# Six of eight head chunks for four output tiles inside the attention

## The chip, the cores and the metric

One core of a Trainium2 chip runs one launch of the kernel. The metric is device time in microseconds of that launch. TensorE (PE in the profile) multiplies, VectorE (DVE), ScalarE (ACT) and GpSimd (POOL) do the elementwise work, and SyncE (SP) issues nearly all transfers.

## The reference, cut to what matters

A transformer block over 512 tokens of width 1024, in float32. Sixteen heads of 64 are computed in two halves: eight "NSA" heads (a compressed, a selected and a window branch with gates) and eight heads with a window of 128 and a sink. Their outputs are joined, multiplied by an output matrix and normed into the residual; a gated MLP with a short convolution and a gated side input follow.

```python
h = rmsnorm(x, attn_pre_g)
proj = h @ w_in                                   # queries, keys, values, gates
o_nsa = nsa_attention(...)                        # heads 0..7,  (512, 512)
o_swa = swa_attention(...)                        # heads 8..15, (512, 512)
mix = concatenate([o_nsa, o_swa]) @ w_o           # (512, 1024) @ (1024, 1024)
x = x + rmsnorm(mix, attn_post_g)
h = rmsnorm(x, mlp_pre_g)
a, u = split(h @ w_gate_up)                       # 2 * 2816 columns
y = (gelu(causal_dwconv(a)) * u) @ w_down
x = x + rmsnorm(y, mlp_post_g)
x = x + (p @ w_ple) * sigmoid(x @ w_ple_gate)
```

The product with `w_o` is the one that the change touches: 8 tiles of 128 output features, each a sum over 8 chunks of 128 head dimensions (two heads).

## The kernel before, in words

Activations stand transposed, features on the partitions and the 512 tokens along the row. A float32 operand is split into a high and a low part, and every product of a 128x128 weight block with 128x512 activations takes three matmuls: high by high, high by low, low by high. A weight comes from memory through one of two raw buffers (`raw`, the transfer at line 133), ScalarE copies its high part (line 121), and VectorE or POOL subtracts for the low part (line 125). Converted weights live in six slots named `wh`, so three weights fit.

The attention runs in 16 units: eight NSA units (two groups of heads, four blocks of 128 queries each, in the order 3, 0, 2, 1) and then eight window units in the same order. Each step of the loop in `attention` computes the scores of unit `i` together with the product with the values of an earlier unit: of the unit before where that one is NSA, two back where it is a window unit. Its output is put into a pair of head chunks by `put_out`. So chunks 0 to 3 are complete at the end of step 8, chunks 4 and 5 at the end of step 13, and 6 and 7 after the last unit.

Into this go fillers: generators, each step of which is one chunk (three matmuls) of a product that can be done ahead. The attention's generators yield a nominal time in ns for each step; `fill` adds that time multiplied by a rate to a credit, and every 650 ns of credit (`FILL_STEP`) buys one filler step. The rate is taken from `RATES` by the kind of the unit: 0.36 for both NSA groups, 0.9 and 0.6 for the window groups. A filler's first matmul is pinned not to come earlier than an attention matmul six back (`LAG`). The fillers are the remaining projections (six of them, eight steps each) and then `out_proj_first`, which starts when step 8 is done: for all eight output tiles it multiplies chunks 0 to 3 (`mixmm`, lines 775 to 777) and ScalarE saves the sum (line 791). What is left when the units are over is run then. The order on each engine is worked out once by the framework's scheduler, from the program's order and its own timeline, and is fixed when the kernel runs.

`out_proj` adds the rest. For tiles 0 to 2, chunks 4 and 5 are multiplied first, since they cover the wait for the last unit's output, then chunks 6 and 7. Tiles 3 to 7 follow with one weight each, 512 columns (chunks 4 to 7), in PSUM tiles of the tag `mm`, which has two. VectorE adds each finished sum to the saved one (line 820), ScalarE squares it, POOL sums the squares; for the last tile VectorE does (line 230). At tile 2 the weights of the side input are loaded, at tile 4 the four input transfers of 512 KB (line 234), which SP issues in program order, and at tile 7 the first four gate-up weights. Then `norm_add` sets four tiles of the side product, column sums over the squares (line 201), two tiles, the transposition of the norm's factor, two more tiles; the MLP's first matmuls come behind them.

## Time and profile before

| What | us |
|---|---|
| median of 3 runs (lowest, highest) | 677.31 (676.53, 678.64) |
| the profiled execution | 677.48 |
| its span, first to last instruction | 675.7 |
| PE busy | 662.6 (98%) |
| PEld, weight loads, busy | 550.8 (82%) |
| DVE, ACT, POOL busy | 404.1, 324.8, 171.7 |

The granted TensorE clock is 0.998 of full speed over the span. Times in the rows are us from the span's start. In a row of the timeline the bracket holds the time that the engine sat idle before the instruction, and what released it. A matmul's own length overlaps the next one's, so distances between starts tell more than lengths. In names, `fill_` stands for fillers, `nsa_` and `swa_` for the two kinds of units, `outproj_` for the product behind the attention; the tiles of head chunks carry the names of the stage in which they were allocated.

### The profile page before, as it was taken

How to read it: one execution, taken by the hardware profiler on the slowest of the kernel's cores; microseconds unless marked ns; L12 is line 12 of the kernel's file. 1: busy time of each engine (PE TensorE's matmuls, PEld its weight loads, DVE VectorE, ACT ScalarE, POOL GpSimd, SP SyncE). 2: the span in 40 equal slices, each digit the busy share in tenths (PEclk: the TensorE clock that was granted, in tenths of full speed). 3: DMA queues.
4: the chain of work that ended last, by engine and by line, in shares of the span. 5: the costliest groups of instructions: out<-in, count | busy, mean ns of one | idle time of the engine just before them, and what ended most of it. 6: DMA issues, size and time to landing. Idle time of an engine off the chain costs nothing.

```text
span 675.7 us, 9173 instructions
## 1 busy us (share of the span) xinstructions
PE 662.6 (98%) x3273; PEld 550.8 (82%) x3273; DVE 404.1 (60%) x809; ACT 324.8 (48%) x602; POOL 171.7 (25%) x244
## 2 busy tenths in 40 slices
PE   8999999999999999999999999999999999999996
PEld 7988868877788777788888888888888888889985
DVE  6785877877657668668645455555542333324872
ACT  7554787877778555454333343433332322222341
POOL 1112577756656234312011110101010000001000
PEclk9999999999999999999999999999999999999999
DMA  8437523101122641122223222222233344232031
GB/s 296 169 105 226 158 63 78 33 16 49 48 83 99 233 146 63 64 93 95 99 107 105 95 94 93 94 94 95 96 97 103 116 121 136 86 99 82 1 124 63
DMA packets 24972, 69.55 MB, mean 103 GB/s; under 512 B 3168, under 2 KB 4448, under 8 KB 24928
## 3 DMA queue, kind: packets, MB, share of 16 engines
q1 hardware_dynamic: 24784, 68.89, 31.4%
q8 instruction: 26, 0.43, 0.3%
q14 instruction: 18, 0.15, 0.1%
q10 hardware_dynamic: 144, 0.08, 0.0%
HBM read 59.52 MB, written 2.10 MB: 91 GB/s over the span
## 4 chain that ended last, share of the span: by engine, by line
PE 89%; DVE 4%; ACT 3%; DMA 2%; issue 1%; ACTq 0%; DVEq 0%
PE mlpup_pss L144 5%; PE mlpup_pss L143 4%; PE mlpup_pss L140 4%; PE mlpup_psmm L143 3%; PE mlpup_psmm L140 3%; PE mlpup_psmm L144 3%; PE nsa_pso L541 3%; PE mlpup_pst L143 3%; PE mlpup_pst L140 3%; PE mlpup_pst L144 3%; PE mlpdown_pss L144 3%; PE mlpdown_pss L140 3%; PE mlpdown_pss L143 3%; PE nsa_pst L508 2%; PE mlpdown_psmm L140 2%; PE mlpdown_psmm L144 2%
## 5 line engine op out<-in xcount | busy, mean ns | idle before, releaser
L121 ACT ACTIVATE mlpup_wh<-mlpup_wr 128x1024 fp32r<-128x1024 f32 x40 | 42.5, 1063 | 82.2 <-PE mlpup_pss L143 30.3
L924 POOL TENSOR_TENSOR mlpup_s<-mlpup_s,r3b 128x512 f32<-128x512 f32 x22 | 29.4, 1339 | 186.6 <-ACT mlpup_s L923 186.6
L125 DVE TENSOR_TENSOR mlpdown_wh<-mlpdown_wr,mlpdown_wh 128x1024 fp32r<-128x1024 f32 (+1 forms) x28 | 33.1, 1181 | 59.8 <-ACT mlpdown_wh L121 59.8
L121 ACT ACTIVATE mlpdown_wh<-mlpdown_wr 128x1024 fp32r<-128x1024 f32 (+1 forms) x28 | 28.0, 1000 | 84.8 <-PE mlpdown_pss L143 33.1
L125 DVE TENSOR_TENSOR mlpup_wh<-mlpup_wr,mlpup_wh 128x1024 fp32r<-128x1024 f32 x40 | 50.6, 1265 | 9.2 <-ACT mlpup_wh L121 9.1
L140 PE MATMUL mlpup_pss<-r_u,mlpup_wh 128*128 128x512 f32 x120 | 46.8, 390 | 0.0
L144 PE MATMUL mlpup_pss<-r_u,mlpup_wh 128*128 128x512 f32 x120 | 46.7, 389 | 0.0
L143 PE MATMUL mlpup_pss<-r_u,mlpup_wh 128*128 128x512 f32 x120 | 46.7, 389 | 0.0
L530 POOL TENSOR_SCALAR nsa_u<-nsa_u,nsa_nrc,gate 128x512 f32<-128x512 f32 (+3 forms) x64 | 38.2, 607 | 22.5 <-DVE nsa_nrc L655 16.7
L624 ACT ACTIVATE nsa_u<-nsa_u,nsa_nnm 128x512 f32<-128x512 f32 (+3 forms) x64 | 35.5, 557 | 5.2 <-DVE nsa_nnm L620 4.9
L512 DVE TENSOR_TENSOR nsa_u<-nsa_pst,nsa_u 128x512 fp32r<-128x512 f32 (+1 forms) x43 | 29.0, 683 | 9.1 <-ACT nsa_u L510 8.8
L230 POOL TENSOR_TENSOR mlpdown_s<-mlpdown_s,mlpdown_s 128x512 f32<-128x512 f32 x6 | 7.8, 1298 | 100.4 <-ACT mlpdown_s L229 100.4
L620 DVE CUSTOM_DVE_ANT_0 nsa_u<-nsa_pss,biastables_u 128x512 f32<-128x512 f32 (+3 forms) x64 | 29.9, 486 | 5.3 <-PE nsa_pss L562 4.9
L125 POOL TENSOR_TENSOR fill_wh<-fill_wr,fill_wh 128x512 fp32r<-128x512 f32 (+1 forms) x14 | 24.7, 1762 | 32.9 <-ACT fill_wh L121 32.8
L144 PE MATMUL mlpdown_pss<-mlpup_u,mlpdown_wh 128*128 128x512 f32 (+1 forms) x88 | 32.0, 364 | 0.0
L140 PE MATMUL mlpdown_pss<-mlpup_u,mlpdown_wh 128*128 128x512 f32 (+1 forms) x88 | 32.0, 364 | 0.0
L143 PE MATMUL mlpdown_pss<-mlpup_u,mlpdown_wh 128*128 128x512 f32 (+1 forms) x88 | 32.0, 363 | 0.0
L510 ACT ACTIVATE nsa_u<-nsa_pst 128x512 fp32r<-128x512 f32 (+1 forms) x43 | 25.1, 592 | 13.0 <-PE nsa_pst L508 12.7
L923 ACT ACTIVATE mlpup_s<-mlpup_s 128x512 f32<-128x512 f32 x22 | 13.8, 633 | 36.2 <-DVE mlpup_s L922 36.2
L140 PE MATMUL mlpup_pst<-r_u,mlpup_wh 128*128 128x512 f32 x80 | 31.2, 390 | 0.0
L144 PE MATMUL mlpup_pst<-r_u,mlpup_wh 128*128 128x512 f32 x80 | 31.1, 389 | 0.0
L143 PE MATMUL mlpup_pst<-r_u,mlpup_wh 128*128 128x512 f32 x80 | 31.1, 389 | 0.0
(411 smaller groups left out, 1979.1 us busy)
## 6 DMA issues: line engine op xcount, KB each, us to landing
mlpup_wr<-in_gu_dram SPq DMA_DIRECT2D x40, 512.0 KB, 3.2
mlpdown_wr<-in_down_dram SPq DMA_DIRECT2D x16, 512.0 KB, 3.5
fill_wr<-in_win_dram SPq DMA_DIRECT2D x6, 512.0 KB, 3.6
mlpdown_wr<-in_down_dram SPq DMA_DIRECT2D x8, 384.0 KB, 3.1
fill_u<-fill_u SPq DMA_DIRECT2D x20, 128.0 KB, 2.4
loadx_u<-in_xT_dram SPq DMA_DIRECT2D x8, 256.0 KB, 4.8
compress_u<-projk_u SPq DMA_DIRECT2D x16, 128.0 KB, 2.3
fill_wr<-in_wo_dram SPq DMA_DIRECT2D x8, 256.0 KB, 2.9
```

Of the source, the lines that this page charges most:

```text
L121: h = nc.scalar.activation(hi, raw, AF.Copy)
L125: l = eng.tensor_sub(lw, raw, hi.bitcast(F32))
L140: r = self.pin(mm(ps, hi, x[:, 0, :], start=start, stop=False))
L143: mm(ps, lo, x[:, 0, :], start=False, stop=False)
L144: mm(ps, hi, x[:, 1, :], start=False, stop=stop)
L510: nc.scalar.activation(t[:rows, 0, :], pt[:rows], AF.Copy)
L512: nc.vector.tensor_sub(lo, pt[:rows], t[:rows, 0, :].bitcast(F32))
L530: self.nc.gpsimd.tensor_scalar(ap, ap, col, gate, op0=ALU.mult, op1=ALU.mult)
L541: self.att(nc.tensor.matmul(po, v, rhs, start=start, stop=stop))
L620: nc.vector.tensor_tensor_reduce(dst, src, dist, op0=ALU.add, op1=ALU.min, scale=SLOPES[8 + 4 * g + r], scalar=3e38, accum_out=nm[:, r, b ...
L624: nc.scalar.activation(dst, dst, AF.Exp, bias=nm[:, r, b : b + 1], scale=-1.0, accum_out=sm[:, r, b : b + 1])
L924: nc.gpsimd.tensor_mul(c0, c0, self.r3)
```

## The change

- A table `BORDER` gives the rates of steps 6, 7 and 8: 0.36, 0.7 and 0.9. Step 7 is the last NSA unit.
- `out_proj_first` takes a range of tiles and a number of chunks. Tiles 0 to 3 (`SIX` = 4) still take four chunks, from the end of step 8; tiles 4 to 7 take six, as a second filler that is appended at the end of step 13 (`NQT * 3 + 1`), when chunks 4 and 5 are complete. Weights of the second are 768 columns wide.
- In `out_proj`, tiles 4 to 7 multiply only chunks 6 and 7. Their weights, four times 256 columns, come in one transfer into one raw buffer when tile 4 is reached, are converted as one weight of 1024 columns, and each tile takes its part. `raw` lays the destination out in as many pieces as the source has.

```diff
--- before.py
+++ after.py
@@ -55,6 +55,8 @@
 FILL_STEP = 650.0
 WARM = 9
 RATES = [0.36, 0.36, 0.9, 0.6]
+BORDER = {6: .36, 7: .7, 8: .9}
+SIX = 4
 LAG = 6
 
 
@@ -130,7 +132,7 @@
 
     def raw(self, src, n=1024, tag="wr"):
         t = (self.wrp.tile([P, n], F32, tag="wr", name=self.nm("wr")) if tag == "wr" else self.u([P, n], F32, tag))
-        self.nc.sync.dma_start(t, src)
+        self.nc.sync.dma_start(t if len(src.shape) == 2 else t.rearrange("p (c n) -> p c n", c=src.shape[1]), src)
         return t
 
     def mm3(self, ps, wt, off, x, start, stop, keep=False):
@@ -743,7 +745,7 @@
                         self.drain(qf[f])
                 if mix[k] is None:
                     mix[k] = self.mix_tiles()
-                self.rate = RATES[k]
+                self.rate = BORDER.get(i, RATES[k])
                 u["mix"] = mix[k]
                 if u["kind"] == "n":
                     gens.append((self.nsa_scores(u), [(j + 1) / 8 for j in range(8)]))
@@ -758,13 +760,16 @@
                 self.mix = []
                 for k in range(2):
                     self.mix += [(mix[k][0][:, i, :], mix[k][1][:, i, :]) for i in range(2)]
-                self.fillers.append(self.out_proj_first())
+                self.mo = [self.u([P, 2, T]) for _ in range(4)]
+                self.fillers.append(self.out_proj_first(range(SIX), 4))
+            if i == NQT * 3 + 1:
+                self.mix += [(mix[2][0][:, k, :], mix[2][1][:, k, :]) for k in range(2)]
+                self.fillers.append(self.out_proj_first(range(SIX, KC), 6))
             if u is not None:
                 before.append(u)
         while self.fillers:
             self.fill_step()
-        for k in range(2, 4):
-            self.mix += [(mix[k][0][:, i, :], mix[k][1][:, i, :]) for i in range(2)]
+        self.mix += [(mix[3][0][:, k, :], mix[3][1][:, k, :]) for k in range(2)]
 
     def mixmm(self, ps, wt, ks, n0=0, end=True):
         mm = self.nc.tensor.matmul
@@ -777,18 +782,16 @@
             mm(ps, lo, xh, start=False, stop=end and n == last)
             yield
 
-    def out_proj_first(self):
-
-        nc, io = self.nc, self.io
-        self.mo = [self.u([P, 2, T]) for _ in range(4)]
-        w = lambda c: self.weight(io["wo"][c][:, : 4 * P], 4 * P, lo="pool")
-        wts = [w(0)]
-        for c in range(KC):
-            if c + 1 < KC:
-                wts.append(w(c + 1))
+    def out_proj_first(self, cs, n):
+
+        w = lambda c: self.weight(self.io["wo"][c][:, : n * P], n * P, lo="pool")
+        wts = [w(cs[0])]
+        for i, c in enumerate(cs):
+            if i + 1 < len(cs):
+                wts.append(w(cs[i + 1]))
             ps = self.ps("mm")
-            yield from self.mixmm(ps, wts[c], range(4))
-            nc.scalar.activation(self.mo[c // 2][:, c % 2, :], ps, AF.Copy)
+            yield from self.mixmm(ps, wts[i], range(n))
+            self.nc.scalar.activation(self.mo[c // 2][:, c % 2, :], ps, AF.Copy)
 
     def out_proj(self):
         self.phase = "outproj"
@@ -811,9 +814,18 @@
                 ps, wt = first[c]
                 run(self.mixmm(ps, wt, range(6, 8), 2, True))
             else:
-                wt = self.weight(io["wo"][c][:, 4 * P :], 4 * P)
+                if c < SIX:
+                    k = 4
+                    wt = self.weight(io["wo"][c][:, k * P :], (KC - k) * P)
+                else:
+                    k = 6
+                    if c == SIX:
+
+                        n = KC - SIX
+                        last = self.weight(io["wo"][SIX:, :, k * P :].rearrange("c p n -> p c n"), n * 2 * P)
+                    wt = [w[:, (c - SIX) * 2 * P : (c - SIX + 1) * 2 * P] for w in last]
                 ps = self.ps("mm")
-                run(self.mixmm(ps, wt, range(4, 8)))
+                run(self.mixmm(ps, wt, range(k, KC)))
             if c == KC - 1:
                 self.upw = [self.weight(io["gu"][i]) for i in range(2)]
             m = self.mo[c // 2][:, c % 2, :]
```

## Rows read from the trace of the kernel before

**Rows 1.** Windows by stage: length, busy us (count) by engine, clock, DMA

```profile
145.00:181.00 36.00, 34.26 (x197) 27.59 (x195) 28.95 (x110) 29.33 (x87) 23.66 (x46) 1.00 0.16 45
...
181.00:223.60 42.60, 42.02 (x222) 35.12 (x223) 27.24 (x75) 34.85 (x86) 24.16 (x40) 1.00 0.29 93
...
223.60:247.20 23.60, 23.17 (x97) 17.55 (x96) 14.26 (x17) 10.19 (x17) 8.41 (x7) 1.00 0.56 191
...
340.00:360.00 20.00, 20.00 (x90) 16.57 (x89) 11.54 (x14) 7.45 (x10) 1.29 (x1) 1.00 0.27 93
```

**Rows 2.** Timeline of PE, output projection: start, length, instruction, [idle before]

```profile
237.14 0.39 PE L776 MATMUL outproj_psmm<-swa_u,outproj_wh 128*128 128x512 f32 x1
...
237.37 0.39 PE L777 MATMUL outproj_psmm<-swa_u,outproj_wh 128*128 128x512 f32 x1
...
237.88 0.50 PE L775 MATMUL outproj_psmm<-nsa_u,outproj_wh 128*128 128x512 f32 x1
...
238.95 0.39 PE L775 MATMUL outproj_psmm<-nsa_u,outproj_wh 128*128 128x512 f32 x1
...
243.70 0.39 PE L777 MATMUL outproj_psmm<-swa_u,outproj_wh 128*128 128x512 f32 x1
...
244.40 0.47 PE L775 MATMUL outproj_psmm<-nsa_u,outproj_wh 128*128 128x512 f32 x1 [0.31 <-DVE fill_u L820]
```

**Rows 3.** Timeline of PE, matmuls after idle time, 145 to 181

```profile
153.80 0.36 PE L561 MATMUL nsa_pss<-compress_u,projq_u 128*128 128x256 f32 x1 [0.61 <-DVE nsa_nnm L620]
...
157.98 0.36 PE L561 MATMUL swa_pss<-projq_u,fill_u 128*128 128x256 f32 x1 [0.38 <-DMA fill_u<-fill_u]
...
161.15 0.74 PE L541 MATMUL nsa_pso<-nsa_u,vnatural_u 128*128 128x512 f32 x2 [0.36 <-ACT nsa_u L510]
...
179.62 0.36 PE L561 MATMUL swa_pss<-projq_u,fill_u 128*128 128x256 f32 x1 [0.34 <-DVE swa_u L512]
```

**Rows 4.** Timeline of PE, window units

```profile
215.29 0.50 PE L775 MATMUL fill_psmm<-projq_u,fill_wh 128*128 128x512 f32 x1 [0.58 <-ACT fill_u L791]
```

**Rows 5.** Timeline of SP's queue, then the chain of waits

```profile
225.45 1.46 SPq L133 DMA_DIRECT2D outproj_wr<-in_wo_dram  x2
...
226.97 1.86 SPq L234 DMA_DIRECT2D outproj_u<-in_xT_dram  x4
...
229.49 7.62 DMA outproj_wr<-in_wo_dram
```

**Rows 6.** Groups by form: busy us, mean ns, idle before

```profile
L125 POOL TENSOR_TENSOR fill_wh<-fill_wr,fill_wh 128x512 fp32r<-128x512 f32 x8 | 10.3, 1290 | 9.7 <-ACT fill_wh L121 9.6
...
L125 POOL TENSOR_TENSOR fill_wh<-fill_wr,fill_wh 128x1024 fp32r<-128x1024 f32 x6 | 14.4, 2392 | 23.3 <-ACT fill_wh L121 23.3
...
L121 ACT ACTIVATE outproj_wh<-outproj_wr 128x1024 fp32r<-128x1024 f32 x4 | 4.2, 1057 | 3.5 <-DMA outproj_wr<-in_gu_dram 3.5
...
L125 DVE TENSOR_TENSOR outproj_wh<-outproj_wr,outproj_wh 128x1024 fp32r<-128x1024 f32 x4 | 4.9, 1225 | 2.9 <-ACT outproj_wh L121 2.9
...
L820 DVE TENSOR_TENSOR fill_u<-fill_u,outproj_psmm 128x512 f32<-128x512 f32 x7 | 4.8, 680 | 2.4 <-PE outproj_psmm L777 2.4
```

**Rows 7.** Timeline of PE and of ACT at the fifth tile

```profile
234.88 0.39 PE L775 MATMUL outproj_psmm<-nsa_u,outproj_wh 128*128 128x512 f32 x1
...
231.35 0.62 ACT L121 ACTIVATE outproj_wh<-outproj_wr 128x512 fp32r<-128x512 f32 x1
```

**Rows 8.** DMA issues: count, KB each, median us to landing

```profile
mlpup_wr<-in_gu_dram SPq DMA_DIRECT2D x40, 512.0 KB, 3.2
...
loadx_u<-in_wv_dram SPq DMA_DIRECT2D x8, 204.0 KB, 4.8
```

**Rows 9.** Timeline of DVE and PE behind the output projection

```profile
250.67 0.69 DVE L230 TENSOR_TENSOR outproj_s<-outproj_s,outproj_s 128x512 f32<-128x512 f32 x1 [0.83 <-ACT outproj_s L229]
...
252.77 0.95 PE L201 MATMUL r_pst<-ones,outproj_s 128*128 128x1 f32 x8
```

## The prediction

> **What bounds the kernel now.** I read the stage windows first, then TensorE's idle time before single matmuls, then the chain of waits through the output projection, then the conversions and transfers that stand in that chain. The windows show TensorE busy in every stage: 34.26 of 36.0 us where the last compressed units meet the first window units (145 to 181), 42.02 of 42.6 in the window units (181 to 223.6), 23.17 of 23.6 in the rest of the output projection (223.6 to 247.2), and all 20.0 us of a plain stretch of the MLP [rows 1]. No other engine is near that, but VectorE with 28.95 and ScalarE with 29.33 of 36 us come closest in the first. So the end is set by how many matmuls there are and by the holes between them; a moved matmul saves nothing unless it lies in a hole.
>
> A busy TensorE is not a full one. The Trainium skill ("Perfetto Trace Analysis", Identifying the Most-Contended Engine) says that the matmul row's busy share misjudges headroom and the share of weight loads should be read instead. The windows bear it out: 16.57 of 20 us in the MLP (0.83), but 0.77, 0.82 and 0.74 in the three stages [rows 1]; an estimate by that page is (0.83-0.77)*36 + (0.83-0.82)*42.6 + (0.83-0.74)*23.6 = 4.7 us of headroom in all. The sum below is made from the holes alone.
>
> The holes, by starts: a 512-column matmul follows another after 0.23 us (237.14 to 237.37) [rows 2].
> - 145 to 181: TensorE idle 0.61, 0.38, 0.36 and 0.34 us before four matmuls, put down to VectorE, a copy of projected queries, ScalarE and VectorE [rows 3]; 1.69 us, and with 0.11 each that the first matmul after an idle stretch loses (0.50 instead of 0.39 long [rows 2, 4]) 2.1.
> - 181 to 223.6: one of 0.58 us, on ScalarE emptying a filler's sums [rows 4]; 0.69 with its restart.
> - Output projection: 237.37 to 237.88 is 0.51 us instead of 0.23; the three matmuls from 237.88 to 238.95 take 1.07 instead of 0.69; 243.70 to 244.40 is 0.70 [rows 2]. That is 0.28 + 0.38 + 0.47 = 1.13 us. The chain says why: the transfer issued at 229.49 holds it for 7.62 us [rows 5], since SP has put four input transfers in front, at 226.97 [rows 5].
>
> **The change, part by part.**
>
> *Chunks moved.* Before, 8 tiles * 4 chunks = 32 filler steps run in the attention and 32 chunks after it. Now 4*4 + 4*6 = 40 and 24. Three matmuls a chunk: 192 in both. 8*3*0.23 = 5.5 us leave the output projection and enter the attention; by itself 0.
>
> *The rate.* Entries 6 and 8 of the new table repeat what RATES gives. Only unit 7 changes. Its nominal 9182 ns pay for 9182*0.36/650 = 5 steps now, for 9 at 0.7. Counted through, units 8 to 17 get 7, 2, 5, 5, 4, 4, 4, 3, 2, 2 steps before and 7 are left after the last unit; after: 8, 1, 6, 5, 4, 1, 6, 3, 2, 2, and 11 left. Four more steps (4*3*0.23 = 2.8 us) lie between 145 and about 165, beside the first three holes. These waits are on other engines, and VectorE's 28.95 of 36 us does not shrink, so a filler fills a hole only if the fixed order puts it just there. The projection awaited at 157.98 also comes earlier, since its last two steps are paid for at twice the rate. Bounds: 0 and -1.35 (the three idle times) - 0.33 (their restarts) = -1.7. I take -1.3, nearer the full gain, because TensorE has more ready work than hole in each place.
>
> *Unit 13.* The 16 steps of the first four tiles run out there: 1 step instead of 4, because the second filler is appended only at its end. 3*0.69 = 2.1 us of cover is missing. What hides it: three steps of unit 12's work and the scheduler's freedom to set a matmul up to six attention matmuls back. Bounds 0 and +2.1; the nearest row is an uncovered wait of 0.34 to 0.61 us [rows 3], so +0.4. The first four chunks of a six-chunk tile need nothing of the third pair's outputs, so no further wait is added.
>
> *End of the attention.* 11 steps instead of 7 remain to stand beside the last window products and their evacuation. The hole of 0.58 us waits on ScalarE, busy 34.85 of 42.6 us [rows 1]; a filler tile now empties once in 18 matmuls instead of 12. Bounds 0 and -0.7; I take -0.4.
>
> *Conversions in the attention.* Four weights grow from 512 to 768 columns. POOL: 1290 ns at 512, 2392 at 1024 [rows 6], so about 1.84, +0.55 us four times, on an engine with 24.16 of 42.6 us used [rows 1]. ScalarE: 0.62 at 512 [rows 7] and 1.06 at 1024 [rows 6], +0.22 four times. Hidden by the 4.1 us of TensorE work that a six-chunk tile brings; without that cover 3.1 us.
>
> *One transfer for the last four tiles.* Five weights (tiles 3 to 7) become two: ScalarE 5*0.62 = 3.1 to 1.7 us, VectorE 5 subtractions to 2. More to the point, the three transfers behind the input loads go; the new one is asked for at tile 4, ahead of them. So the 1.13 us go, if it is in time. Before, tile 4 starts at 234.88, 48 matmuls into the stage, and its weight is converted from 231.35 [rows 7]. Issued by 226.9 as now [rows 5], 512 KB in 1 KB pieces takes between 3.2 us (512 KB in whole rows) and 4.8 (204 KB in 1632-byte rows) [rows 8]: 230.1 to 231.7; ScalarE 1.06 and VectorE 1.23 [rows 6] end at 232.4 to 234.0. One microsecond is left. Bounds of this part: -1.13 and +4 (the second rival); I take -1.1.
>
> *Short tiles.* Tiles 4 to 7 last 6*0.23 = 1.38 us instead of 2.76, in two banks. VectorE's addition takes 0.68 [rows 6]; one gate-up conversion of 1.23 in front makes 1.91, 0.53 more than a tile, but a second bank stands by. Bounds 0 and 4*0.53 = +2.1; I take +0.1. [...] No run here shows a six-matmul tile.
>
> *Behind the projection.* Four side-product tiles stand in TensorE's order between the last projection matmul and the column sums at 252.77; the squares' sum is ready at 250.67 + 0.69 = 251.36 [rows 9]. That leaves 1.4 us of slack, and gate-up conversions that move earlier only ease it. From there on everything shifts as a block: 0.
>
> **Sum.** -1.3 + 0.4 - 0.4 - 1.1 + 0.1 = -2.3 us on the profiled execution of 677.48 (span 675.7 and 1.8 around it): 675.2. The median of the runs is 0.17 lower, 677.31, so 675.0. The likeliest case's own range is 673.8 to 676.0. About 0.3% (2.0 us, below 675.3 or above 679.3) is what a measurement can tell from no change.
>
> **The rivals.**
> 1. *VectorE paces the units around 150 to 160.* Then the four extra steps only push its work back, and the waits reappear one step later; unit 13 costs half of its 2.1. For it: VectorE's high share there [rows 1], and two of the four holes wait on it [rows 3]. Against: between the waits TensorE never runs dry, so it is the one that is behind. 0 + 1.0 - 0.2 - 1.1 = -0.3: 677.0. No change to be seen.
> 2. *Slower: the joined transfer lands behind the input loads.* It is one load for four tiles, and SP is in order; if the raw buffer frees a moment later in the schedule, the four input transfers pass it, as they passed the one that took 7.62 us [rows 5]. It then lands at about 237.1, high half at 238.2, low half at 239.4, while TensorE stands at 234.88: 3.4 us for the first matmul, about 4 with the low half, and no chunks of other tiles lie between. -1.3 + 0.4 - 0.4 + 4.0 = +2.7, 680.0. It decides from a landing later than 234.9 - 1.06 = 233.8. For it: on SP the two stand 0.06 us apart (225.45 + 1.46 and 226.97) [rows 5]. Against: the code asks before the input loads.
> 3. *All holes close*: -(2.1 + 0.7 + 1.1) = -3.9, 673.4. For it: 11 steps at the end. Against: waits between attention steps move rather than vanish.
> 4. *The change does not do what it says*: the six-chunk fillers land after the last window product, as 11 steps can. TensorE's order at the end is then as before and unit 7 and the transfer alone count, which is the sum above less 0.4: 675.4; it is counted with the forecast.
>
> **Chances.** Forecast 0.47 (0.35 of it beyond 0.3%), rival 1 0.26, rival 2 0.15, rival 3 0.12. Faster by over 0.3%: 0.35 + 0.12 = 0.47; within: 0.12 + 0.26 = 0.38; slower: 0.15. The range runs from a microsecond below rival 3, whose restarts are only bounded, to short of rival 2, 672.4 to 678.4; it leaves out 0.05 below and 0.14 above.
>
> **What would show it.** Right: the three holes of the output projection gone, its stage after the last window product about 16.6 us (72 matmuls), one 512 KB output-weight transfer landing before the inputs, at least two of the holes around 153, 158 and 161 gone, a small new one in unit 13, the same distance from the last projection matmul to the first gate-up matmul. Wrong: a wait before tile 4 on ScalarE or the transfer (rival 2); TensorE's idle time in the attention unchanged (rival 1); additions of VectorE holding tiles 6 or 7; the column sums waiting for POOL's sum of squares.

## The result and the profile after

| | before | changed |
|---|---|---|
| median of 16 runs each, us | 677.29 (676.53 to 678.64) | 673.04 (672.21 to 676.40) |
| ratio | | 0.9943, 95% interval 0.9933 to 0.9954 |
| profiled execution, span | 677.48, 675.7 | 676.40, 674.3 |
| the same, changed kernel run again | | 672.74, 670.6 |

The change makes the kernel faster by 0.57%, 4.25 us in the medians; 675.0 was forecast, so the gain came out nearly twice the 2.3 us predicted, inside the range.

The first profile of the changed kernel is of its slowest execution, so I read it beside a second profile of the same kernel (run again among the experiments below). Both begin alike up to the first matmul of the attention units, except that this comes at 72.64 us in the first, and at 70.59 us in the second and 70.70 before; the last section tells of that. From there the stages are compared by their length. They are cut at the first attention matmul, the first window scores, the last product of the compressed units, the first plain output matmul, the last one, and the first up-projection matmul. Before (length, then busy us and count of PE, PEld, DVE, ACT, POOL, the clock, DMA share, GB/s):

```profile
70.70:157.12 86.42, 84.87 (x463) 66.41 (x461) 69.13 (x278) 69.88 (x186) 60.03 (x93) 1.00 0.26 72
157.12:180.49 23.37, 22.25 (x131) 18.02 (x129) 17.64 (x58) 17.92 (x55) 13.92 (x32) 1.00 0.16 41
180.49:223.63 43.14, 42.56 (x224) 35.39 (x224) 27.75 (x77) 35.39 (x87) 24.70 (x42) 1.00 0.29 92
223.63:247.21 23.58, 23.15 (x97) 17.55 (x96) 14.26 (x17) 10.17 (x17) 8.38 (x7) 1.00 0.56 191
247.21:259.76 12.55, 12.55 (x62) 10.10 (x60) 7.63 (x10) 8.47 (x14) 2.80 (x2) 1.00 0.46 164
```

The changed kernel, second profile:

```profile
70.59:159.00 88.41, 87.50 (x475) 68.61 (x473) 69.93 (x277) 71.12 (x190) 62.27 (x97) 1.00 0.27 72
159.00:181.79 22.79, 22.45 (x134) 18.72 (x132) 16.48 (x55) 16.50 (x49) 12.06 (x27) 1.00 0.14 36
181.79:225.82 44.03, 43.93 (x232) 36.84 (x232) 27.88 (x79) 36.21 (x89) 27.42 (x42) 1.00 0.32 102
225.82:242.49 16.67, 16.57 (x74) 13.44 (x72) 10.21 (x14) 8.54 (x13) 5.97 (x6) 1.00 0.66 237
242.49:255.09 12.60, 12.60 (x62) 10.02 (x60) 8.37 (x11) 8.37 (x15) 5.56 (x4) 1.00 0.50 166
```

The changed kernel, first profile, the last two stages (the first three took 88.39, 22.81 and 43.93 us):

```profile
227.77:244.11 16.34, 16.34 (x73) 13.49 (x72) 8.88 (x12) 6.30 (x11) 5.27 (x5) 1.00 0.71 241
244.11:259.01 14.90, 13.04 (x61) 9.94 (x59) 9.74 (x12) 10.69 (x17) 6.24 (x4) 1.00 0.42 142
```

Two things are to be seen. The three attention stages take 155.23 us instead of 152.93, 2.30 more, though 24 matmuls more stand in them, 5.44 us at their pitch of 0.2265; so 3.14 us of holes were filled. The output projection falls by 6.91, of which 5.44 are the matmuls that left and 1.47 its holes. Behind the projection the second profile shows no change (12.60), the first 2.35 us more. The whole of the second profile is 4.74 us shorter than before's in device time and 5.1 us in its span. The five stages make up 4.56 us of that; why the rest of the span is 0.5 us shorter too is open.

The holes themselves: of the idle times of [rows 3] and [rows 4], 2.27 us in all, one of 0.34 us is left in the second profile,

```profile
160.82 1.16 PE L543 MATMUL nsa_pso<-nsa_u,vnatural_u 128*128 128x512 f32 x4 [0.34 <-DVE nsa_s L526]
```

and in the output projection [rows 2] none is left in either. On SP's queue the joined transfer now stands ahead of the inputs, where three weight transfers had stood behind them [rows 5]. Second profile, the queue (start, length, instruction):

```profile
227.10 1.52 SPq L135 DMA_DIRECT2D outproj_wr<-in_wo_dram  x2
228.68 3.10 SPq L236 DMA_DIRECT2D outproj_u<-in_xT_dram  x4
233.52 11.46 SPq L135 DMA_DIRECT2D outproj_wr<-in_gu_dram  x4
```

In the first profile two new waits stood behind the projection, both on VectorE:

```profile
246.99 0.50 PE L142 MATMUL r_psmm<-pletiles_u,pletiles_wh 128*128 128x512 f32 x1 [1.33 <-DVE swa_u L832]
251.97 1.02 PE L203 MATMUL r_pst<-ones,outproj_s 128*128 128x1 f32 x8 [0.53 <-DVE outproj_s L232]
```

Their cause is in the same profile on ScalarE and VectorE. The first gate-up weight landed late, its high half was converted at 244.02, its low half on VectorE at 245.11, and tile 6's addition, which frees the bank for the side products, stood behind that in VectorE's order:

```profile
244.02 1.06 ACT L123 ACTIVATE outproj_wh<-outproj_wr 128x1024 fp32r<-128x1024 f32 x1 [3.80 <-DMA outproj_wr<-in_gu_dram]
```

```profile
245.11 1.23 DVE L127 TENSOR_TENSOR outproj_wh<-outproj_wr,outproj_wh 128x1024 fp32r<-128x1024 f32 x1 [2.83 <-ACT outproj_wh L123]
246.25 0.68 DVE L832 TENSOR_TENSOR swa_u<-swa_u,outproj_psmm 128x512 f32<-128x512 f32 x1
```

In the second profile the same instructions in the same order came soon enough, ScalarE 14.25 us after the first plain output matmul instead of 16.25, and TensorE did not wait:

```profile
240.07 1.06 ACT L123 ACTIVATE outproj_wh<-outproj_wr 128x1024 fp32r<-128x1024 f32 x1 [1.47 <-DMA outproj_wr<-in_gu_dram]
```

### The profile page after: what moved, and what is told of

It reads as the page before. It is cut to its first block, busy times and chain, and to the rows that moved or that the text cites. A ratio compares the mean times of both kernels' runs of the same rounds, so it can differ in the third digit from the quotient of the medians.

```text
span 674.3 us, 9160 instructions
## 1 busy us (share of the span) xinstructions
PE 662.9 (98%) x3273; PEld 553.1 (82%) x3273; DVE 401.0 (59%) x806; ACT 323.3 (48%) x599; POOL 175.2 (26%) x244
## 4 chain that ended last, share of the span: by engine, by line
PE 86%; DVE 5%; DMA 3%; ACT 3%; issue 1%; POOL 1%; ACTq 0%; DVEq 0%; POOLq 0%
PE mlpup_pss L146 4%; PE mlpup_pss L145 4%; PE mlpup_pss L142 4%; PE nsa_pso L543 3%; PE mlpup_pst L146 3%; PE mlpup_pst L145 3%; PE mlpup_psmm L145 3%; PE mlpup_psmm L146 3%; PE mlpup_pst L142 3%; PE mlpup_psmm L142 3%; PE mlpdown_pss L142 3%; PE mlpdown_pss L146 3%; PE mlpdown_pss L145 3%; PE nsa_pst L510 2%; PE mlpdown_psmm L142 2%; PE mlpdown_psmm L146 2%
## 5 line engine op out<-in xcount | busy, mean ns | idle before, releaser
L127 POOL TENSOR_TENSOR fill_wh<-fill_wr,fill_wh 128x1024 fp32r<-128x1024 f32 (+2 forms) x14 | 26.9, 1922 | 26.2 <-ACT fill_wh L123 26.2
L512 ACT ACTIVATE nsa_u<-nsa_pst 128x512 fp32r<-128x512 f32 (+1 forms) x43 | 25.3, 591 | 12.2 <-PE nsa_pst L510 11.8
```

Of the source, the lines that this page charges most:

```text
L127: l = eng.tensor_sub(lw, raw, hi.bitcast(F32))
L512: nc.scalar.activation(t[:rows, 0, :], pt[:rows], AF.Copy)
```

## The experiments

Each ratio is to the kernel before on the same chip. Its median there was 677.51 us for the rate alone, the moved chunks alone, the run without the joined transfer and the one with additions ahead of conversions; 677.31 for the run without output fillers and the three that move the inputs (to tile 7, and behind the gate-up weights with and without the additions first); 677.74 for the changed kernel again, the earlier conversion and the longer warm-up; 677.84 for the spread rate.

**The rate alone.** The kernel before, with unit 7's entry of the table and nothing else.

```diff
+BORDER = {7: .7}
-                self.rate = RATES[k]
+                self.rate = BORDER.get(i, RATES[k])
```

> The kernel before with the one rate alone: 0.7 in the last compressed unit, nothing else. Theory A (the rate fills the holes between 145 and 165 us): those three holes close, 1.3 to 2 us faster than before, and the holes of the output projection stay (1.1 us). Rival B (VectorE paces those units, and the gain in the attention is that of the eight chunks that are moved): the holes reappear a step later, within 0.5 us of before.

Measured: 680.38 us, ratio 1.0049 (1.0025 to 1.0073), slower; neither expectation held. The three attention stages of its profile, which is of the fastest of its nine runs (678.41 us), and TensorE's waits in the last of them:

```profile
70.55:158.92 88.37, 87.45 (x474) 68.61 (x473) 69.94 (x277) 71.20 (x190) 62.53 (x97) 1.00 0.27 72
158.92:181.75 22.83, 22.49 (x134) 18.71 (x132) 16.48 (x55) 16.51 (x49) 12.12 (x27) 1.00 0.13 36
181.75:225.84 44.09, 39.10 (x209) 32.28 (x209) 29.25 (x80) 36.67 (x90) 25.07 (x42) 1.00 0.30 96
```

```profile
209.40 1.16 PE L542 MATMUL swa_pso<-swa_u,vnatural_u 128*128 128x512 f32 x4 [0.99 <-ACT swa_u L589]
219.18 1.14 PE L542 MATMUL swa_pso<-swa_u,vnatural_u 128*128 128x512 f32 x3 [0.58 <-DVE swa_s L525]
224.84 1.16 PE L542 MATMUL swa_pso<-swa_u,vnatural_u 128*128 128x512 f32 x4 [3.41 <-ACT pletiles_wh L122]
```

The two stages ahead of the windows took 88.37 and 22.83 us, as in the changed kernel: 18 filler matmuls more (4.08 us) in 1.41 us more, 2.67 hidden, and three of the four holes of [rows 3] gone. The window units then had 93 filler matmuls instead of 111, and yet took 44.09 us instead of 43.14. The last of their fillers starts 36.45 us into the stage (before: 41.99); behind that the last unit's chain stood open, 3.41 us before the last window product. The trace puts the end of that wait down to a conversion of a side-product weight on ScalarE, of which the product itself needs nothing. But two such conversions stand among the last unit's steps there, the first of them late, and on VectorE the subtraction of the first (222.11, 1.23 us) stands ahead of the additions that end 0.15 us before the product:

```profile
221.02 1.06 ACT L122 ACTIVATE pletiles_wh<-pletiles_wr 128x1024 fp32r<-128x1024 f32 x1 [1.03 <-DMA pletiles_wr<-in_wple_dram]
223.70 1.05 ACT L122 ACTIVATE pletiles_wh<-pletiles_wr 128x1024 fp32r<-128x1024 f32 x1
```

So two things meet there: no filler was left to cover the chain, and conversions made it longer. How the 3.41 us divide between them no run shows. Whether the dry end is the cause at all, or the units need 43 to 44 us whatever lies between, two of the runs below tell.

The 2.9 us of the medians are more than the profile explains, which is 0.8 us longer in its span (2.36 more in the attention; 1.36 less in the projection, where the weight transfers behind the inputs were issued 3.64 us after its first matmul instead of 5.85). In four of the nine runs, 682.0 to 684.3 us, the granted clock over the whole run was 0.991, in the other five 0.996 to 0.998, so a part of the 2.9 us goes with TensorE's clock.

**The moved chunks alone.** The changed kernel without its table; the joined transfer stays.

```diff
-BORDER = {6: .36, 7: .7, 8: .9}
+BORDER = {}
```

> The changed kernel with the rate of the last compressed unit back at 0.36. Theory A: 1.3 to 2 us slower than the changed kernel, with the holes around 153, 158 and 161 back. Rival B: within 0.5 us of the changed kernel.

Measured: 679.41 us, ratio 1.0020 (1.0005 to 1.0034), slower. Its window stage and, in the projection behind it, a wait:

```profile
180.42:229.00 48.58, 48.33 (x248) 40.17 (x248) 28.43 (x79) 36.64 (x87) 27.86 (x43) 1.00 0.28 93
```

```profile
245.97 0.50 PE L780 MATMUL outproj_psmm<-swa_u,outproj_wh 128*128 128x512 f32 x1 [1.85 <-DVE swa_u L832]
```

All 24 matmuls fell into the window units, and these grew by 48.58 - 43.14 = 5.44 us, the matmuls' own pitch: there TensorE was full. The holes around 153, 158 and 161 are back, as expected (0.61, 0.30 and 0.36 us), but the price is not the 1.3 to 2 us expected: the profile is 6.6 us longer than the changed kernel's second. The attention is 3.00 us longer, the projection 2.03, most of it the 1.85 us on an addition, and the stage behind it 1.27 (last section).

**Rate and chunks, without the joined transfer.** The changed kernel with a weight transfer of its own for each of the last four tiles.

```diff
-                    if c == SIX:
-                        n = KC - SIX
-                        last = self.weight(io["wo"][SIX:, :, k * P :].rearrange("c p n -> p c n"), n * 2 * P)
-                    wt = [w[:, (c - SIX) * 2 * P : (c - SIX + 1) * 2 * P] for w in last]
+                    wt = self.weight(io["wo"][c][:, k * P :], (KC - k) * P)
```

> The changed kernel, but each of the last four tiles loads and converts its own 256 columns (four transfers of 128 KB instead of one of 512 KB); the order on TensorE is the same. Theory A (the joined transfer pays because it stands ahead of the input transfers): the weights of tiles 6 and 7, for which no raw buffer is free before, land behind the inputs, TensorE waits for them, 1 to 3 us slower than the changed kernel. Rival: short tiles need only small weights, the raw buffers turn over quickly, and it is within 0.5 us.

Measured: 675.09 us, ratio 0.9958 (0.9944 to 0.9973). The projection took 17.82 us, with one wait of 0.42 us on ScalarE's conversion of an output weight, instead of 16.67 and 16.34. Rate and chunks together give -2.4 us in these medians, and with the joined transfer -4.25 in the medians of the result. The rate alone gives +2.9, and the chunks with the joined transfer but without the rate +1.9: the two parts need each other. The joined transfer adds 1.1 to 1.5 us in the projection; in the medians (0.9943 against 0.9958) the intervals overlap.

**The window units without output fillers.** The kernel before, with its output filler offered only behind all units.

```diff
-                self.fillers.append(self.out_proj_first())
+        self.fillers.append(self.out_proj_first())   # behind the loop over units
```

> The kernel before with the output-projection filler offered only behind all attention units, so the window units are without output matmuls among them. Theory (the window units have a length of their own, set by their chain through ScalarE, VectorE and GpSimd, and fillers lie in their holes for nothing until TensorE is full): the stretch from the last product of the compressed units to the first plain output matmul stays at 42 to 45 us with about 111 filler matmuls fewer, and those matmuls come behind it at their full pitch, 24 us more in all. Rival (the window units are paced by TensorE): the stretch falls by the matmuls taken out, to 20 to 25 us, and the whole time stays near 677.

Measured: one run, 689.44 us. Its window stage:

```profile
182.38:224.53 42.15, 38.21 (x191) 29.58 (x191) 23.44 (x68) 30.54 (x78) 22.63 (x38) 1.00 0.14 42
```

The edit did not do all it says: the scheduler set the output fillers back among the later window units, so that they begin at 207 us instead of 187 (but for one step at 176), and only 33 matmuls fewer stand in the stage, not 111. Its length says nothing by itself then, but its first part does. The seventeenth of its 30 products starts 20.56 us into it with 18 fillers in front, where before it is 27.21 us with 72: 54 fillers, 12.2 us at their pitch, cost 6.6. So about half of them lay in holes, and the units did not need the time: the theory of a fixed length, 42 to 45 us, is not borne out by this, though the total fell into its range.

**The rate alone, spread.** The first run with the rates of the window units lowered, so that their fillers last to the end.

```diff
-RATES = [0.36, 0.36, 0.9, 0.6]
+RATES = [0.36, 0.36, 0.7, 0.45]
```

> The run with the rate alone, with the rates of the window units lowered from 0.9 and 0.6 to 0.7 and 0.45, so that the fewer fillers left for them last to the last unit: 99 filler matmuls in the window stage in place of 93 there and 111 before, with 12 of them in the last tenth, as before, in place of none. Theory A (that run lost because its fillers ran dry ahead of the last window unit, whose chain then stood open): the window stage falls below that of before by some of the 12 matmuls taken out, to 40.5 to 42 us, the 3.4 us wait ahead of the last window product is gone, and the kernel is 1 to 2 us faster than before, 675.5 to 676.5. Theory B (the window units have a length of their own, 42 to 44 us, whatever lies between): the stage stays at 43 to 44.5 with the waits elsewhere in it, and the time is 678 to 680.

Measured: 678.06 us (677.57 to 681.36, twelve runs), ratio 1.0008 (0.9994 to 1.0021): no change. The profile is of an execution near the upper end, 681.14. Its window stage:

```profile
183.97:225.01 41.04, 40.20 (x209) 32.77 (x210) 26.23 (x71) 33.30 (x81) 23.06 (x39) 1.00 0.29 89
```

41.04 us instead of 44.09, with 99 fillers instead of 93: theory A holds for the stage's length, B falls, and the wait of 3.41 us is gone. But the spread changed one thing more. The side-product weights are now converted behind the start of the last window product instead of ahead of it:

```profile
224.01 1.17 PE L542 MATMUL swa_pso<-swa_u,vnatural_u 128*128 128x512 f32 x4 [0.41 <-DVE swa_s L525]
224.78 1.05 ACT L122 ACTIVATE pletiles_wh<-pletiles_wr 128x1024 fp32r<-128x1024 f32 x1
```

What of the 3.05 us is due to that order is not told apart. The gain of 1 to 2 us on the whole did not come. With the compressed units at 23.04 the three attention stages took 152.41 us, only 0.52 less than before; and in this execution the projection lost 2.4 us more than before's, on a conversion of an output weight whose transfer stands behind the inputs, and on TensorE's clock behind that wait (last section).

Five kernels now give the length of the three attention stages:

| fillers in them | window rates | length, us |
|---|---|---|
| 240, before | 0.9, 0.6 | 152.93 |
| 240, unit 7 faster | 0.9, 0.6 | 155.29 |
| 240, unit 7 faster | 0.7, 0.45 | 152.41 |
| 264, unit 7 as before | 0.9, 0.6 | 158.23 |
| 264, the change | 0.9, 0.6 | 155.23 |

The rate alone makes these stages 2.36 us longer, the moved chunks alone 5.30, nearly the full pitch of their 24 matmuls (5.44), and both together 2.30. So once unit 7 is faster, the 24 matmuls cost nothing (155.29 and 155.23): the changed kernel has none of the waits of 0.99, 0.58 and 3.41 us that the rate alone leaves in the window units. Against the best kernel with 240 fillers, 152.41, they cost 2.82. Each length is of one profile; the first profile of the changed kernel has 155.13, and five other runs here with the same attention and no wait of their own in it have 155.07 to 155.17.

**The projection's holes of before.** The kernel before, its four input transfers issued at tile 7 instead of 4.

```diff
-            if c == 4:
+            if c == 7:
```

> The kernel before with one edit: the four input transfers of the residual are issued at output tile 7 in place of tile 4, so on SyncE's queue they stand behind the last output weights and the first two gate-up weights. TensorE's order is that of before. Theory (the holes of before in the output projection, 1.1 to 1.8 us in all, are waits for weight transfers that share the engines with the four inputs): the holes close, 1.1 to 1.8 us faster, about 675.8 against 677.5. Rival (the weights' conversions on ScalarE and VectorE set the holes, the transfers only stand near): no change, 677 to 678. Second rival (the inputs land too late for the first normalised sum behind the projection): slower by up to 2 us.

Measured: 677.59 us, ratio 0.9999 (0.9987 to 1.0010), no change. The projection took 22.12 us, 1.46 less: the transfers behind the inputs were the cause of its holes, as predicted. But the stage behind it took 13.58 instead of 12.55, with a wait that has taken their place:

```profile
257.73 0.65 PE L214 MATMUL r_pst<-ident,r2c 128*128 128x128 f32 x4 [0.83 <-POOL r2c L207]
```

GpSimd's operation waited for a small one of VectorE at 255.44, and that stood behind the conversion of a gate-up weight which had landed late, as in the changed kernel's first profile. A closed hole moved to the next late transfer. This profile also had the late start, so that the gain which is left, 0.4 us, can't be told in the medians.

**Additions ahead of conversions.** The changed kernel, VectorE's additions of tiles 4 to 7 held in their order and the gate-up conversions behind them.

```diff
-            if c == KC - 1:
-                self.upw = [self.weight(io["gu"][i]) for i in range(2)]
-            nc.vector.tensor_add(m, m, ps)
+            r = nc.vector.tensor_add(m, m, ps)
+            if c >= SIX:
+                self.tc.keep_in_program_order(r)
+            if c == KC - 1:
+                self.upw = [self.weight(io["gu"][i], keep=True) for i in range(2)]
```

> The changed kernel, with VectorE's additions for the last four output tiles kept ahead of the conversions of the first gate-up weights; the orders on TensorE and of the transfers are the same. In the changed kernel TensorE idles 1.33 us at 247 because VectorE waits at 242.3 to 245.1 for the first gate-up weight's conversion with the addition of tile 6 queued behind it, and 0.53 us at 252. Theory A (the order on VectorE is the cause): both holes close, 1.5 to 2.2 us faster than the changed kernel. Rival C (the side product's bank or the sum of squares on POOL is late by itself): the hole stays or moves to the column sums, within 0.5 us. Rival D: the gate-up weights become late for the MLP's first matmuls, 0 to 2 us slower.

Measured: 674.53 us, ratio 0.9951 (0.9934 to 0.9967). The waits of 1.33 and 0.53 us are gone, but now the last two gate-up conversions come late, and others stand behind them:

```profile
256.08 0.50 PE L142 MATMUL mlpup_pss<-r_u,outproj_wh 128*128 128x512 f32 x1 [0.78 <-ACT r_u L874]
257.37 0.50 PE L146 MATMUL mlpup_pss<-r_u,outproj_wh 128*128 128x512 f32 x1 [0.56 <-DVE r_u L883]
```

13.94 us behind the projection, between the two profiles of the changed kernel. A gain over the changed kernel is not shown (its ratio is 0.9943, and the intervals overlap).

**The inputs behind the gate-up weights,** on top of that run.

```diff
-            if c == 4:
-                for j in range(4):
-                    ... (the four input transfers)
+        for j in range(4):   # behind the loop over tiles and the four gate-up weights
+            ... (the four input transfers)
```

> The run with the additions ahead of the gate-up conversions, with one more edit: the four input transfers are issued behind the four gate-up weights. TensorE's order stays. Theory (what is lost behind the output projection is the late gate-up weights, which wait on SyncE's queue behind the inputs, and whose conversions hold up ScalarE's evacuations): the stretch from the last output matmul to the first up-projection matmul falls from 13.9 to about 12.6 us, and the time by about 1.3 us, to some 673.2 with a start like that run's. Rival (the inputs become the late thing: the sum for the norm needs the first of them at about 254.6 us): the stretch stays at 13.9 or grows, the time 674.5 or more.

Measured: 673.91 us, ratio 0.9953 (0.9941 to 0.9965); 13.54 us behind the projection. The theory's 1.3 us did not come, only 0.4: the gate-up weights share two raw buffers, so that the later two still wait until the first are converted. Its window stage was 0.85 us longer, with a wait of 0.69 us on a transfer inside the attention that no other run shows there.

**The inputs behind the gate-up weights, alone.** The same edit on the changed kernel.

> The changed kernel with one edit: the four input transfers behind the four gate-up weights on SyncE's queue; the order of additions and conversions on VectorE stays. Theory (the queue is the root: VectorE's gate-up conversion waits because the weight lands late, and the addition of tile 6 waits behind it): the 1.33 and 0.53 us holes behind the output projection mostly close, the stretch from the last output matmul to the first up-projection matmul falls from 14.9 to 12.6 to 13.2 us, 1.5 to 2.2 us faster than the changed kernel. Rival (the order on VectorE is the root, since the conversion itself of 1.23 us stands ahead of the addition): the hole shrinks by no more than a third, under 0.7 us gained.

Measured: 673.39 us, ratio 0.9950 (0.9937 to 0.9964). Behind the projection 12.54 us, as before the change; but the projection took 17.29, since a conversion now stood ahead of tile 4's addition on VectorE:

```profile
238.91 0.50 PE L780 MATMUL outproj_psmm<-swa_u,outproj_wh 128*128 128x512 f32 x1 [0.67 <-DVE swa_u L832]
```

That fits the theory that the queue's order makes the conversions late, but the ratio shows no gain over the changed kernel, and what the edit would gain depends on which profile of that kernel it is held against, so:

**The changed kernel again.** No edit.

> The changed kernel itself once more, beside the next runs on the same chip. Theory (its one profiled run had a start 1.9 us later than that of before, with the same instructions up to there, and the rest of its profile is typical): the median stays at 672.5 to 674; a profiled run with the first attention matmul near 70.7 us shows the same holes behind the output projection, 14.9 us from its last matmul to the first up-projection matmul, and a span near 672. Rival (the holes behind the projection belong to that one execution): 12.5 to 13 us there, a span near 670.

Measured: 674.40 us (672.67 to 675.25, six runs), ratio 0.9946 (0.9930 to 0.9962). The rival holds: 12.60 us behind the projection, span 670.6; the median lies above the theory's 672.5 to 674. So the edit ahead does not show what the queue's order is worth, the waits there belong to single executions, and the three runs on the order of conversions and inputs were partly aimed at a cause that this execution does not have. How many have it is open: of the 22 runs of this kernel twelve took 672.2 to 673.6 us, as this profile's did, and ten 674.3 to 676.4.

**First conversion one tile earlier.** The run with additions first and inputs behind the gate-up weights, with the first gate-up weight converted behind tile 6's addition.

```diff
-            if c == KC - 1:
-                self.upw = [self.weight(io["gu"][i], keep=True) for i in range(2)]
+            if c >= KC - 2:
+                self.upw = (self.upw if c == KC - 1 else []) + [self.weight(io["gu"][c - KC + 2], keep=True)]
```

> The run with the additions first and the inputs behind the four gate-up weights, with one more edit: the first gate-up weight is converted behind tile 6's addition in place of tile 7's. TensorE's order stays. Theory (what that run still lost behind the projection, 13.5 against 12.5 us, was the last gate-up conversion on VectorE ahead of the norm, one step late because the raw buffers come free late): 12.5 to 12.7 us there with 16.3 us in the projection, 0.9 us faster than that run and 2.3 us faster than the changed kernel in this stretch. Rival (the conversion ahead of tile 7's addition delays the column sums): 13.0 to 14 us, no gain.

Measured: 672.58 us (672.45 to 674.36, six runs), ratio 0.9929 (0.9915 to 0.9944). Both last stages:

```profile
225.85:242.17 16.32, 16.32 (x73) 13.52 (x72) 9.78 (x14) 8.50 (x14) 6.96 (x7) 1.00 0.34 113
242.17:254.71 12.54, 12.54 (x61) 10.10 (x59) 9.59 (x11) 8.35 (x14) 4.13 (x3) 1.00 0.69 232
```

No wait above 0.1 us is left in either (one of 0.47 us follows in the MLP); this is the fastest kernel of the study by its median. Against the changed kernel on the same chip (0.9946) the intervals overlap, and its profile is 0.14 us shorter (672.60 and 672.74), so a gain over the change is not shown.

**More warm-up.** The changed kernel with 14 matmuls at the start for 9.

```diff
-WARM = 9
+WARM = 14
```

> The changed kernel with 14 warm-up matmuls at the start in place of 9. Theory (the first real matmuls wait for their data until 6.3 us, and the spread of the runs, 4 us, comes from whether TensorE has risen to its higher rate by then): longer warm-up keeps it busy, the first attention matmul comes at about 70.7 us in the profile, and the runs spread by less than 2 us around 672.5. Rival (the warm-up already lasts until the data is there): the start is later by the five matmuls, 1 to 2 us, and the median 674 to 675.

Measured: 674.86 us (674.20 to 675.27, five runs), ratio 0.9955 (0.9941 to 0.9968). The spread is down to 1.1 us, as the theory said, but at the upper end, as the rival said, though not by its reason: the first real matmul comes at 6.54 us and all run at full pitch, and the time is lost later, in waits of 0.76 us at 37.48 and 0.43 us at 46.55 on VectorE that the other profiles don't have. Why more warm-up brings these is open.

## Why the prediction was right or wrong

- **The sum itself: its terms are not independent.** The time lies in the range, but neither half of the sum holds by itself. The rate, -1.3 in the sum, alone made the kernel slower by 2.9 us; all the other terms, +0.4 - 0.4 - 1.1 + 0.1 = -1.0, without the rate made it slower by 1.9. Only together they gain, so that the sum came near is in part luck. The rate does close the holes that it was meant for, and hides 2.67 us of fillers, but it takes six filler steps out of the window units (I had counted four) and these run dry; the moved chunks put eight back.
- **Chunks moved, "by itself 0".** 24 matmuls go to the attention, and I charged them there at their full pitch. With the old rates that is right, 5.30 of 5.44 us. With the rate raised they cost nothing, and against the spread rates 2.82, so how much of the gain is theirs and how much the rate's can't be said.
- **The size in the attention: -1.3 forecast (the rate -1.3, unit 13 +0.4, the end -0.4), -3.14 measured.** The named idle times of [rows 3, 4] shrank by 1.93 us; with 0.11 for each of the four that are gone, the price that I had set for a restart, that makes 2.4, an estimate, where I took 1.7. Unit 13 cost nothing that is seen, where I took 0.4. The remaining 0.8 us lay in gaps too short for a row to name: the windows' busy share, 42.02 of 42.6 [rows 1], had made me think that no such room was left.
- **Unit 13, +0.4, and the end of the attention, -0.4.** No wait is seen at either place; the wait of 0.58 us [rows 4] is gone. The last compressed units and the windows, taken together since two other matmuls changed from the one to the other, took 66.82 us instead of 66.51 with 12 fillers more (2.72 us).
- **One transfer, -1.1, and short tiles, +0.1: right.** 1.47 and 1.80 us of holes closed in the two profiles, more than the 1.13 that I had named: the stage of before is 1.84 us longer than its 96 matmuls at their pitch. The transfer took 5.2 and 4.8 us to land, longer than my 3.2 to 4.8, and was in time all the same. Separate transfers cost 1.15 to 1.5 us there. Each addition took 0.68 us and had its tile of 1.36; no halved group made TensorE wait in the changed kernel's projection.
- **Behind the projection, 0: right for the second profile (+0.05), wrong for the first (+2.35).** The slack of 1.4 us [rows 9] had been read for the column sums alone; "gate-up conversions that move earlier only ease it" was wrong, since they move earlier in VectorE's order, not on the wire, and a late one holds up an addition. That price, one conversion in front of an addition, I had put at 0.53 us for tiles in the projection.
- **The rivals.** The third, all holes closed, 673.4, at a chance of 0.12, is what happened in size, and by more than its 3.9 us in the second profile. Its argument against, that waits between attention steps move rather than vanish, was wrong for the change; with the rate alone they did come back later, as 4.98 us in the window units. The first, VectorE as the pace, fell: 0.34 us of waits are left. The second, the late joined transfer, fell. The fourth fell too: the fillers lie before the last window product.
- **The time around the span.** I took 1.8 us around the span, as before; in the two profiles of the changed kernel it is 2.1. Why is open.
- **The rule on weight loads.** The estimate of 4.7 us by the Trainium skill ("Perfetto Trace Analysis", Identifying the Most-Contended Engine) came nearer to the 4.56 us gained over the five stages than the forecast's 2.3 or the 3.9 of all named holes did. Whether the rule or chance did it, one case can't tell, and the shares did not stop at the MLP's 0.83: PEld's share rose to 18.72 of 22.79 and 36.84 of 44.03 us, 0.82 and 0.84, but in the projection only to 0.81.

## What to carry to other kernels

A change of how much filler there is and a change of where it is handed out are one change: price them together, and look whether the fillers run dry before the last unit that they cover, or pile up in one stage. Named idle times are not all the holes: compare a stage's length with its instructions at their pitch too. Take a second execution's profile before explaining a new wait, and where an in-order engine converts a late weight just ahead of an operation that others need, put that operation in front.

## What the runs showed of the hardware

TensorE's clock fell behind waits in the projection. In the run with the rate spread, after 1.58 us of idle time, and then the stretch behind it:

```profile
240.85 0.50 PE L776 MATMUL outproj_psmm<-nsa_u,outproj_wh 128*128 128x512 f32 x1 [1.58 <-ACT outproj_wh L122]
```

```profile
240.50:246.00 5.50, 5.15 (x14) 3.79 (x15) 2.41 (x4) 2.19 (x4) 1.28 (x1) 0.69 0.48 136
```

The granted clock is 0.69 in it, matmuls start 0.43 us apart, the level of 1.2 GHz for 512 columns, instead of 0.23, and from 246 on it is 1.00 again: behind the wait of 1.58 us this cost another 1.6 (the nine starts from 242.38 to 246.02 take 3.64 us, at 0.2265 they would take 2.04). The run with the chunks alone shows the same 0.69 in the 4.3 us after its projection, which ended soon after the wait of 1.85 us; that is why its stage behind the projection took 13.87. The run without output fillers shows 0.69 from 249.0 to 254.5, behind a wait of 2.53 us. The waits of 1.33 us (the changed kernel's first profile) and of 3.41 (the rate alone) were followed by 1.00. What makes the difference is open.

TensorE also starts in two ways, with the same instructions. In the first profile of the changed kernel, after nine warm-up matmuls and 0.59 us of idle time:

```profile
6.32 0.71 PE L349 MATMUL vnatural_pss<-loadx_u,loadx_u 128*128 128x408 f32 x1 [0.59 <-ACT loadx_u L323]
6.83 0.54 PE L350 MATMUL vnatural_pss<-loadx_u,loadx_u 128*128 128x408 f32 x1
7.17 0.54 PE L349 MATMUL vnatural_pss<-loadx_u,loadx_u 128*128 128x408 f32 x1
```

In the second, after nine and 0.66 us:

```profile
6.33 0.46 PE L349 MATMUL vnatural_pss<-loadx_u,loadx_u 128*128 128x408 f32 x1 [0.66 <-ACT loadx_u L323]
6.62 0.34 PE L350 MATMUL vnatural_pss<-loadx_u,loadx_u 128*128 128x408 f32 x1
6.80 0.34 PE L349 MATMUL vnatural_pss<-loadx_u,loadx_u 128*128 128x408 f32 x1
```

Starts are 0.34 us apart in the one, which for 408 columns is the level of 1.2 GHz, and 0.18 in the other, near that of 2.4. The windows of the profile give a granted clock of 1.00 for both stretches, but in the first profile nothing was recorded there: the trace's records of the clock begin at 10.8 us (in the second profile at 5.5), and time without a record counts as 1.00. The slow stretch lasts until about 10.6 us and costs 1.9 us. Of the thirteen profiles with nine warm-up matmuls five show it, three of kernels built on before and two built on the change, so it is no effect of the change. In these five the clock's records begin between 10.2 and 10.9 us, in the other eight between 4.4 and 6.4. Only one run of each kernel leaves a trace, so how much of each median it makes up is open; it may be why the medians differ by 3.3 to 4.3 us and the two profiles with the early start by 4.74.
